# The second pointwise product of a Conformer layer: high and low activations side by side in one 512-column product, and two sums in the epilogue

## The chip, the core and the metric

The kernel runs as one program on one core of one Trainium2 chip. The metric is device time in microseconds (us), the median of the runs shown. A profile is one execution of the program, recorded by the hardware profiler.

The engines are written as in the profile: PE is TensorE (matmul), PEld its weight load, DVE is VectorE, ACT is ScalarE, POOL is GpSimd, SP issues the large DMAs. L189 is line 189 of the kernel's file before the change.

## The reference, cut to what matters

The reference is a backbone of two layers over 256 latent tokens and 256 context tokens of width 1024. Layer 0 mixes tokens with a Conformer convolution module, layer 1 with a bidirectional mLSTM; a squared-ReLU MLP follows each. The change is in the last line of the convolution module and the sum that follows it:

```
a = jax.nn.silu(layer_norm(a + b_dw, ln_g, ln_b))
return a @ w_pw2 + b_pw2                            # conformer_conv
...
h = layer_norm(ALPHA * h + g1 * y, ln1_g[i], ln1_b[i])
h = layer_norm(ALPHA * h + g2 * sq_relu_mlp(modulate(h, sh2, sc2), mlp_w1[i], mlp_w2[i]), ln2_g[i], ln2_b[i])
```

`a @ w_pw2` has 512 tokens in two streams (s = 0, the context, and s = 1, the latent tokens), 1024 inputs and 1024 outputs. The gate `g1` differs by stream.

## The kernel before, in words

**Layout.** Activations lie channel-first: a tile holds 128 channels in its partitions and the 512 tokens of both streams in its columns. `LO` is columns 0 to 255 and `HI` columns 256 to 511. `x[f]` (f = 0 to 7) is the residual.

**Splitting.** A product in full float32 precision is made from three products of a reduced type. `split` (L153) writes the high part of a value (a cast on ACT, L154) and the low part, the value less its high part (DVE, L155). `mm3` (L184) then issues three matmuls into one PSUM tile: high weight by high activation (L185), high weight by low activation (L188), low weight by high activation (L189). One output block of 128 channels over 1024 inputs is 8 k-tiles, so 24 matmuls.

**The stage of the change.** `silu` (L1112) makes the product's input for one stream: for each k-tile f two transposes on PE into a PSUM bank (L1119), the SiLU on ACT (L1122), a cast and a subtraction. The high part goes into columns `LO` of a tile of 512 columns and the low part into `HI` of the same tile (L1124, L1125); `sact[s]` keeps the two halves as a pair (L1126).

`gemm2_steps` (L292) makes the product, stream by stream, with eight output blocks m for each. In stream 0 the first four (`ko=4`) are made together, k-tile by k-tile, in halves of two banks opened ahead (L310 to L323). The other twelve, m = 4 to 7 of stream 0 and m = 0 to 7 of stream 1, are made one after the other (L324 to L330), each in one of the three banks with the tag "mm", of which it uses 256 columns. The weights are split once and kept: m = 0 to 3 in the tiles `wh` and `wl`, m = 4 to 7 in tiles of the pool "hid".

The epilogue `pw2_epi` (L1180) adds gate times product to the residual on DVE (L1181). It then feeds the result to the layer norm of that stream (`Norm`, L494): sums on DVE (L508, L510, L536, L538, L540), one early mean on PE (L514), a shift by it (L530), squares on ACT (L535). After the last block, `finish` (L543) makes the statistics: small matmuls on PE (L548, L551), a few tiny DVE instructions (L553 to L561), a square root on ACT (L558) and transposes on PE (L564). `apply` (L567) and `affine_half` (L588) then make the MLP's input `uu`, for each f two adds on DVE (L569, L570), two activations on ACT (L592) and a subtraction on DVE (L593).

The MLP's first product (`mlp`, L1195) runs through `gemm2_steps` as well, stream 0 first with three blocks together (`ko=3`), six blocks for each stream. Its inputs are the halves `LO` of `uu` for stream 0 and `HI` for stream 1. Its epilogue is L1202, L1203 and a split.

**What sets the order.** The text of the kernel doesn't set the order on an engine alone. The framework's scheduler orders each engine's instructions ahead of the run, by priorities and its own estimate of when operands are ready, unless an instruction is tied by hand (`tc.issue_after`, `tc.keep_in_program_order`). In this stage nothing on PE is tied, apart from a few statistics. The order is then fixed in the program: on the chip an engine waits at an instruction whose operands aren't there.

Of the kernel before, what the change touches and what calls it, by code (L numbers as in the profile page):

```python
# [12 lines left out]
ALU = mybir.AluOpType  # L13
# [8 lines left out]
C = 256  # L22
# [49 lines left out]
def hybrid_kernel(ctx: ExitStack, tc: tile.TileContext, xT, vecs_d, taps_d, bdw_d, ada0_w, ada_w, wg_d, pw1a, pw1, pw2, w1_0, w2_0,  # L72
                  w1_1, w2_1, up_x, up_z, wv, wo, bo_d, wk, wq, wqT, wdown, rows_d, out):
    nc = tc.nc
# [10 lines left out]
    def nm(s):  # L85
        uid[0] += 1
        return f"{s}_{uid[0]}"
# [3 lines left out]
    def tmp(tag, dt=F32):  # L91
        return tp.tile([P, T], dt, tag=tag, name=nm(tag), bufs={"E": 4, "S": 2, "L": 2, "F": 1}[tag])
# [8 lines left out]
    def psum(tag="mm"):  # L101
        return pp.tile([P, 512], F32, tag=tag, name=nm(tag), bufs={"mm": 3, "ln": 2, "fl": 1, "cv": 2}[tag])
# [16 lines left out]
    def V(name, i=0, n=1):  # L119
        o = _OFF[name][0]  # L120
        return vecs[:, o + i:o + i + n]
# [24 lines left out]
    def raw_load(src):  # L146
        raw = wp.tile([P, 2048], F32, tag="raw", name=nm("raw"), bufs=3)
        loaded[0] = nc.sync.dma_start(raw[:, :src.shape[-1]], src).ins
        return raw
# [3 lines left out]
    def split(hi, lo, src):  # L153
        c = nc.scalar.copy(hi, src)  # L154
        lastsub[0] = nc.vector.tensor_tensor(lo, src, hi.bitcast(F32), op=ALU.subtract).ins  # L155
        return c.ins
# [4 lines left out]
    def split_w(src, make=None):  # L161
        n = src.shape[-1]
        if make is not None:
            his, los = [], []
            for i in range(0, n, T):
                his.append(make(F32R))
                los.append(make(F32R))
                split(his[-1], los[-1], src[:, i:i + T])
            return his, los
        hi = wp.tile([P, 1024], F32R, tag="wh", name=nm("wh"), bufs=NW)[:, :n]  # L170
        lo = wp.tile([P, 1024], F32R, tag="wl", name=nm("wl"), bufs=NW)[:, :n]
        anchors.append(split(hi, lo, src))
        return hi, lo
# [10 lines left out]
    def mm3(ps, wh, wl, xh, xl, start, stop):  # L184
        a = nc.tensor.matmul(ps, wh, xh, start=start, stop=False)  # L185
        if pin[0]:
            tc.keep_in_program_order(a)
        nc.tensor.matmul(ps, wh, xl, start=False, stop=False)  # L188
        lastmm[0] = nc.tensor.matmul(ps, wl, xh, start=False, stop=stop).ins  # L189
# [3 lines left out]
    def mm_any(ps, wh, wl, r, start, stop):  # L193
# [10 lines left out]
        todo[0](start, False)  # L204
        todo[1](False, stop)

    def joined(ps):
        n = ps.shape[-1] // 2
        t = tmp("E")
        nc.scalar.copy(t[:, n:2 * n], ps[:, n:])  # L210
        nc.vector.tensor_tensor(t[:, :n], ps[:, :n], t[:, n:2 * n], op=ALU.add)
        return t[:, :n]
# [7 lines left out]
    def kcol(w, kt):  # L220
        if isinstance(w[0], list):
            w, kt = (w[0][kt // 4], w[1][kt // 4]), kt % 4
        return w[0][:, kt * P:(kt + 1) * P], w[1][:, kt * P:(kt + 1) * P]
# [64 lines left out]
    def gemm2(*a, **k):  # L288
        for _ in gemm2_steps(*a, **k):
            pass  # L290

    def gemm2_steps(w_ap, groups, rhs, order, epi, keep, ko=0, pre=None, again=None, two=None):  # L292

        ws = dict(pre or {})
        raws = {}

        def weights_of(m):
            if m not in ws:  # L300
                g = groups[m // 2]
                if g not in raws:
                    raws[g] = raw_load(w_ap[g, 0])
                ws[m] = split_w(raws[g][:, (m % 2) * 1024:(m % 2 + 1) * 1024], keep if m >= NW else None)
            return ws[m]

        for i, (s, sl) in enumerate(order):
            r = [(h_[:, sl], l_[:, sl]) for h_, l_ in rhs] if not isinstance(rhs, dict) else rhs[s]
            k0 = ko if i == 0 else 0
            if k0:  # L310
                if two:
                    pss = [two[m // 2][:, HALVES[m % 2][1]] for m in range(k0)]
                else:
                    pss = [psum("mm" if m < 3 else "cv")[:, :C] for m in range(k0)]
                for m in range(k0):
                    weights_of(m)
                for kt in range(8):
                    for m in range(k0):
                        mm3(pss[m], *kcol(ws[m], kt), *r[kt], kt == 0 and (not two or m % 2 == 0),
                            kt == 7 and (not two or m % 2 == 1))  # L320
                for m in range(k0):
                    epi(m, pss[m], s, sl)
                yield  # L323
            for m in again if i and again else range(k0, 2 * len(groups)):  # L324
                w = weights_of(m)
                ps = psum()[:, :C]
                for kt in range(8):
                    mm3(ps, *kcol(w, kt), *r[kt], kt == 0, kt == 7)
                epi(m, ps, s, sl)
                yield  # L330
# [138 lines left out]
    def ad(l, s, which):  # L469
        i = ["sh1", "sc1", "g1", "sh2", "sc2", "g2"].index(which)  # L470
        return ada[l][:, i * DT:(i + 1) * DT, s]
# [18 lines left out]
    LO, HI = slice(0, C), slice(C, T)  # L490
# [130 lines left out]
    x, u = [], []  # L621
# [98 lines left out]
    def silu():  # L720
        for i in range(2):
            keep(nc.vector.tensor_tensor(cs[:, :, 14 + i], sgc[:, i * DT:(i + 1) * DT], cc[:, i * DT:(i + 1) * DT],
                                         op=ALU.mult))
# [5 lines left out]
    two = lambda c: et[:, c:c + 2 * (HL + 1)].rearrange("p (i k) -> p i k", i=2)  # L729
# [268 lines left out]
    def apply_norm(pair, h):  # L998
        mv = pair_mv[pair]
        y, z = [Y[2 * pair + i][h] for i in range(2)]  # L1000
        nc.scalar.activation(y, y, AF.Identity, scale=mv[:, 0, 2:3], bias=mv[:, 0, 3:4])
        mark["norm", pair, h] = nc.vector.tensor_scalar(z, z, mv[:, 1, 2:3], mv[:, 1, 3:4],
                                                        op0=ALU.mult, op1=ALU.add).ins
# [106 lines left out]
    sact = {0: [], 1: []}  # L1110

    def silu(s):  # L1112
        apply_norm(s, 0)
        for f in range(DT):
            if f % 2 == 0:
                tr = psum("ln")
                for i in (1, 3, 0, 2):
                    k = f + i // 2
                    mark["turn", k] = nc.tensor.transpose(tr[:, i * P:(i + 1) * P],  # L1119
                                                          Y[2 * s + i % 2][k // 4][:, k % 4 * P:k % 4 * P + P], ident).ins  # L1120
            y = tmp("S")[:, LO]
            nc.scalar.activation(y, tr[:, f % 2 * C:f % 2 * C + C], AF.Silu, scale=V("cln_g", f),  # L1122
                                 bias=V("cln_b", f))
            t = U(F32R)  # L1124
            cast = split(t[:, LO], t[:, HI], y)  # L1125
            sact[s].append((t[:, LO], t[:, HI]))  # L1126
            if f == 0:
                with tc.issue_after(cast):
                    apply_norm(s, 1)
            yield  # L1130

    for _ in silu(0):
        pass
# [27 lines left out]
    def ln1_half(s, sl):  # L1161

        lnp[s].finish()
        if not cab:
            cab.extend(comb(0, "ln1_g0", "ln1_b0", "sc2", "sh2"))
        if s == 0:
            for f in range(DT):
                uu.append((U(F32R), U(F32R)))
                affine_half(uu[f][0][:, sl], uu[f][1][:, sl], lnp[s].apply(f), s, *cab, f)
        else:  # L1170
            uside.append(ln1_rest(sl))
# [6 lines left out]
            yield  # L1178

    def pw2_epi(m, ps, s, sl):  # L1180
        nc.vector.scalar_tensor_tensor(x[m][:, sl], ps, ad(0, s, "g1")[:, m:m + 1], x[m][:, sl],  # L1181
                                       op0=ALU.mult, op1=ALU.add)
        lnp[s].feed(x[m][:, sl])
        if m == 2 * 4 - 1:
            ln1_half(s, sl)
# [134 lines left out]
    for f in range(0, DT, 2):  # L1320
        t = tmp("S")
# [116 lines left out]
    def queries(h):  # L1438
        qq = []

        def q_epi(m, ps):
            if m < 2:
                flush()
            t = qd.tile([P, 2, QW], F32R, tag="qq", name=nm("qq"), bufs=8)
            split(t[:, 0, :C], t[:, 1, :C], joined(ps))
            split(t[:, 0, C:], t[:, 1, C:], rk[:, 4 * h + m, :])
            qq.append((t[:, 0, :], t[:, 1, :]))

        for i, _ in enumerate(gemm_steps(wq, range(2 * h, 2 * h + 2), xcl, T, q_epi, pre=preq)):
            if i % 2:  # L1450
                ada_n2.step()
        return qq
# [230 lines left out]
    for i in range(2):  # L1683
        rx = raw_load(xl_dr[i].rearrange("p b c -> p (b c)"))
        for j in range(8):
            t = XL(F32R)
# [325 lines left out]
    for c in range(4):  # L2012
# [25 lines left out]
        for k2 in range(4):  # L2038
            raw = raw_load(w2_1[4 * c + k2])
            for i in range(2):  # L2040
                kt = 2 * k2 + i
# [3 lines left out]
                w = split_w(raw[:, i * 1024:(i + 1) * 1024])  # L2045
                w = [[w_[:, sl] for sl in HF] for w_ in w]
# [6 lines left out]
        if last:  # L2053
# [13 lines left out]
            for q, sl in HALVES:  # L2067
                ps = psum()[:, :C]
# [103 lines left out]
```

## Time and profile before

| | |
|---|---|
| median of 3 runs | 1655.14 us (1654.32 to 1655.25) |
| the profiled execution's own time | 1655.04 us |
| its span, first to last instruction | 1653.3 us |
| PE busy | 1642.4 us, 99% of the span |
| PEld busy | 1353.4 us, 82% |
| DVE busy | 1066.2 us, 64% |
| ACT busy | 727.7 us, 44% |
| granted TensorE clock | 0.999 |

The last 1.7 us of the profiled execution's time lie around the span. Matmuls are pipelined: a matmul's recorded duration is longer than the distance to the next one, so the cost of a matmul in a stream of them is the distance from start to start. The stage of the change lies between 176 and 216 us of the span.

### The profile page before, as it was taken

What the parts mean: (1) busy time and instruction counts of PE and PEld (TensorE: products, weight loads), DVE (VectorE), ACT (ScalarE), POOL (GpSimd) and SP (SyncE); (2) the same over time, 40 slices, a digit from 0 to 9 for tenths busy, and PEclk for the clock granted to TensorE, in tenths of its full rate; (3) what the DMA queues carried; (4) which work ended last, traced back from release to release, by engine and by line L of the source; (5) the groups of instructions that cost most, each with busy time, mean ns of one, the idle gap of its engine ahead of it and who ended that gap; (6) DMA issues with size and microseconds to landing.
All of it is one profiled execution on the core that took longest, in us unless ns stands there. A gap on an engine that the chain in (4) does not pass through costs nothing.

```text
span 1653.3 us, 22664 instructions
## 1 busy us (share of the span) xinstructions
PE 1642.4 (99%) x8794; PEld 1353.4 (82%) x8794; DVE 1066.2 (64%) x1916; ACT 727.7 (44%) x1170; POOL 15.2 (1%) x67
## 2 busy tenths in 40 slices
PE   9999999999999999999999999999999999999998
PEld 6675998888888998877787899888888888878886
DVE  7786895656535776762254753553489776776677
ACT  4313662232324475641133533442478654555453
POOL 0000000000000000000000000000000000000001
PEclk9999999999999999999999999999999999999999
DMA  9766223444324066557775852553466555674552
GB/s 355 254 212 247 90 78 112 153 141 141 120 98 153 17 229 195 185 196 277 279 243 158 290 179 88 178 191 143 149 228 223 209 211 203 241 293 178 179 195 86
DMA packets 80204, 305.81 MB, mean 185 GB/s; under 512 B 11964, under 2 KB 30304, under 8 KB 50016
## 3 DMA queue, kind: packets, MB, share of 16 engines
q1 hardware_dynamic: 57632, 288.07, 49.4%
q10 hardware_dynamic: 22464, 16.30, 3.2%
q8 instruction: 69, 1.13, 0.3%
q14 instruction: 39, 0.32, 0.1%
HBM read 286.47 MB, written 17.86 MB: 184 GB/s over the span
## 4 chain that ended last, share of the span: by engine, by line
PE 98%; DVE 1%; ACT 0%; issue 0%; DVEq 0%
PE mm L185 18%; PE mm L188 17%; PE mm L189 17%; PE mm L200 7%; PE mm L216 4%; PE mm L218 4%; PE mm L217 4%; PE mm L201 4%; PE cv L216 2%; PE cv L218 2%; PE cv L217 2%; PE fl L342 2%; PE cv L967 1%; PE ln L185 1%; PE ln L217 1%; PE ln L188 1%
## 5 line engine op out<-in xcount | busy, mean ns | idle before, releaser
L155 DVE TENSOR_TENSOR wl<-raw,wh 128x1024 fp32r<-128x1024 f32 x344 | 418.7, 1221 | 246.6 <-ACT wh L154 244.6
L154 ACT CAST wh<-raw 128x1024 fp32r<-128x1024 f32 x344 | 358.7, 1051 | 478.5 <-PE mm L188 271.9
L188 PE MATMUL mm<-u,wh 128*128 128x512 f32 (+1 forms) x802 | 289.0, 360 | 0.0
L185 PE MATMUL mm<-u,wh 128*128 128x512 f32 (+1 forms) x674 | 240.9, 358 | 0.0
L189 PE MATMUL mm<-u,wl 128*128 128x512 f32 (+1 forms) x674 | 238.7, 354 | 0.0
L188 PEld LDWEIGHTS mm<-u,wh 128*128 128x128 f32 x802 | 151.5, 189 | 22.9 <-issue 1.1
L185 PEld LDWEIGHTS mm<-u,wh 128*128 128x128 f32 x674 | 127.3, 189 | 23.9 <-issue 5.1
L189 PEld LDWEIGHTS mm<-u,wl 128*128 128x128 f32 x674 | 127.4, 189 | 17.7
L216 PE MATMUL mm<-wh,xl 128*128 128x512 f32 x256 | 101.0, 395 | 0.1
L185 PE MATMUL mm<-xm,wh 128*128 128x512 f32 x256 | 101.0, 394 | 0.0
L217 PE MATMUL mm<-wh,xl 128*128 128x512 f32 x256 | 100.0, 391 | 0.0
L189 PE MATMUL mm<-xm,wl 128*128 128x512 f32 x256 | 99.7, 390 | 0.0
L218 PE MATMUL mm<-wl,xl 128*128 128x512 f32 x256 | 99.2, 391 | 0.1
L185 PE MATMUL mm<-hid,wh 128*128 128x512 f32 (+1 forms) x256 | 93.3, 365 | 0.0
L189 PE MATMUL mm<-hid,wl 128*128 128x512 f32 (+1 forms) x256 | 92.8, 363 | 0.0
L188 PE MATMUL mm<-hid,wh 128*128 128x512 f32 (+1 forms) x256 | 92.8, 363 | 0.0
L200 PE MATMUL mm<-x,wh 128*128 128x512 f32 x232 | 81.1, 398 | 0.0
L188 PE MATMUL mm<-qq,wh 128*128 128x272 f32 x256 | 73.9, 289 | 0.0
L185 PE MATMUL mm<-qq,wh 128*128 128x272 f32 x256 | 73.5, 289 | 0.0
L189 PE MATMUL mm<-qq,wl 128*128 128x272 f32 x256 | 73.5, 288 | 0.0
L1226 DVE SCALAR_TENSOR_TENSOR x<-mm,ada,x 128x256 f32<-128x256 f32 x64 | 28.5, 480 | 63.7 <-PE mm L189 63.7
L200 PE MATMUL mm<-u,wh 128*128 128x512 f32 x192 | 68.6, 398 | 0.0
(567 smaller groups left out, 3274.6 us busy)
## 6 DMA issues: line engine op xcount, KB each, us to landing
raw<-w SPq DMA_DIRECT2D x64, 1024.0 KB, 4.8
raw<-wo SPq DMA_DIRECT2D x32, 1024.0 KB, 4.8
raw<-ada_w SPq DMA_DIRECT2D x23, 1024.0 KB, 5.2
ar<-ada_w SPq DMA_DIRECT2D x80, 256.0 KB, 3.9
raw<-wv SPq DMA_DIRECT2D x16, 1024.0 KB, 7.0
raw<-wqT SPq DMA_DIRECT2D x16, 1024.0 KB, 5.8
raw<-wq SPq DMA_DIRECT2D x16, 1024.0 KB, 5.2
raw<-wk SPq DMA_DIRECT2D x16, 1024.0 KB, 4.9
```

The lines of the kernel that those rows point to most:

```text
L154: c = nc.scalar.copy(hi, src)
L155: lastsub[0] = nc.vector.tensor_tensor(lo, src, hi.bitcast(F32), op=ALU.subtract).ins
L185: a = nc.tensor.matmul(ps, wh, xh, start=start, stop=False)
L188: nc.tensor.matmul(ps, wh, xl, start=False, stop=False)
L189: lastmm[0] = nc.tensor.matmul(ps, wl, xh, start=False, stop=stop).ins
L200: todo = [lambda s_, e_: nc.tensor.matmul(ps, wh, r[0], start=s_, stop=e_), lambda s_, e_: nc.tensor.matmul(ps[:, :n], wl, r[0][:, :n], st ...
L201: lambda s_, e_: nc.tensor.matmul(ps[:, :n], wl, r[0][:, :n], start=s_, stop=e_)]
L216: nc.tensor.matmul(ps, xh, wh, start=start, stop=False)
L217: nc.tensor.matmul(ps, xl, wh, start=False, stop=False)
L218: nc.tensor.matmul(ps, xh, wl, start=False, stop=stop)
L342: a = mark_unit[0] = nc.tensor.matmul(ps[32 * j:32 * j + 32], cs[:, kt, 14 - 2 * v:46 - 2 * v], blocks[kt], start=first and kt < 4, stop=l ...
L1226: nc.vector.scalar_tensor_tensor(res[m][:, sl_], p_, g[:, m:m + 1], res[m][:, sl_], op0=ALU.mult, op1=ALU.add)
```

## The change

In twelve of the sixteen outputs the two matmuls by the high weight become one of 512 columns, whose moving operand is the whole tile with the high part on the left and the low part on the right. The low weight by the high part stays a matmul of 256 columns, into the left half of the same bank. An output is then 8 matmuls of 512 and 8 of 256 columns, in the order four wide, eight narrow, four wide. The bank holds two partial sums, in its two halves, which the epilogue adds to the residual by two instructions, one after the other. The four outputs that are made together keep the old form.

```
+    def wide(ps, w, r, start, stop):
+
+        n = r[0][0].shape[-1] // 2
+        seq = [(0, kt) for kt in range(4)] + [(1, kt) for kt in range(8)] + [(0, kt) for kt in range(4, 8)]
+        for i, (low, kt) in enumerate(seq):
+            w_, x_, o_ = kcol(w, kt)[low], r[kt][0], ps
+            if low:
+                x_, o_ = x_[:, :n], ps[:, :n]
+            nc.tensor.matmul(o_, w_, x_, start=start and i == 0, stop=stop and i == 15)
...
                 for kt in range(8):
                     for m in range(k0):
-                        mm3(pss[m], *kcol(ws[m], kt), *r[kt], kt == 0 and (not two or m % 2 == 0),
+                        x_ = r[kt] if len(r[kt]) == 2 else [r[kt][0][:, h_] for h_ in (LO, HI)]
+                        mm3(pss[m], *kcol(ws[m], kt), *x_, kt == 0 and (not two or m % 2 == 0),
...
                 w = weights_of(m)
+                if len(r[0]) == 1:
+                    ps = psum()
+                    wide(ps, w, r, True, True)
+                    epi(m, ps, s, sl)
+                    yield
+                    continue
                 ps = psum()[:, :C]
...
-            sact[s].append((t[:, LO], t[:, HI]))
+            sact[s].append((t,))
...
     def pw2_epi(m, ps, s, sl):
-        nc.vector.scalar_tensor_tensor(x[m][:, sl], ps, ad(0, s, "g1")[:, m:m + 1], x[m][:, sl],
-                                       op0=ALU.mult, op1=ALU.add)
+        for h_ in (LO, HI)[:ps.shape[-1] // C]:
+            nc.vector.scalar_tensor_tensor(x[m][:, sl], ps[:, h_], ad(0, s, "g1")[:, m:m + 1], x[m][:, sl],
+                                           op0=ALU.mult, op1=ALU.add)
```

## The prediction

> **What bounds the kernel now.** I read the page's busy shares first, then the chain of work that ended last, then a table of the stage in stretches.
>
> ```profile
> PE 1642.4 (99%) x8794; PEld 1353.4 (82%) x8794; DVE 1066.2 (64%) x1916; ACT 727.7 (44%) x1170; POOL 15.2 (1%) x67
> ...
> PE 98%; DVE 1%; ACT 0%; issue 0%; DVEq 0%
> ```
>
> PE carries 98% of the chain: what a matmul costs in a stream of matmuls is what the kernel costs, unless PE is made to wait. PE and PEld have the same count, so each matmul has its own weight load, also where two in a row use the same weights. The shares are averages, so the stage is read by itself: four blocks of stream 0, blocks 0 to 3 of stream 1, blocks 4 to 7, the MLP's six blocks on stream 0, and the start of its blocks on stream 1.
>
> ```profile
> core 0: us, PE busy (x) PEld busy (x) DVE busy (x) ACT busy (x) POOL busy (x), PEclk, DMA share, GB/s
> 176.28:190.15 13.87, 13.87 (x117) 13.65 (x115) 12.35 (x42) 10.39 (x26) 0.00 (x0) 1.00 0.30 121
> 190.15:203.67 13.52, 13.25 (x111) 12.90 (x109) 10.83 (x29) 8.29 (x13) 0.00 (x0) 1.00 0.14 45
> 203.67:215.69 12.02, 12.02 (x101) 11.95 (x99) 11.52 (x34) 9.24 (x20) 0.00 (x0) 1.00 0.10 40
> 215.69:234.45 18.76, 18.76 (x159) 18.72 (x157) 16.93 (x46) 11.38 (x27) 0.00 (x0) 1.00 0.32 113
> 234.45:246.00 11.55, 11.55 (x99) 11.55 (x98) 11.00 (x26) 8.33 (x17) 0.00 (x0) 1.00 0.10 28
> ```
>
> The columns are the stretch, its length, and each engine's busy time. PE is full but for 0.27 us in the second row. DVE is nearly full too: it has 1.52, 2.69, 0.50, 1.83 and 0.55 us free. So the stage has two engines near their limit, and the change takes work from the one and gives work to the other.
>
> **PE: what a block saves.** The cost of a matmul is the distance from start to start.
>
> ```profile
> 203.67 0.28 PE L185 MATMUL mm<-u,hid 128*128 128x256 f32 x1
> ...
> 206.55 0.28 PE L185 MATMUL mm<-u,hid 128*128 128x256 f32 x1
> ...
> 209.94 0.28 PE L185 MATMUL mm<-u,hid 128*128 128x256 f32 x1
> ...
> 700.02 0.39 PE L185 MATMUL mm<-u,wh 128*128 128x512 f32 x1
> ...
> 703.88 0.39 PE L189 MATMUL mm<-u,wl 128*128 128x512 f32 x1
> ...
> 909.18 0.39 PE L200 MATMUL mm<-u,wh 128*128 128x512 f32 x1
> 909.41 0.27 PE L201 MATMUL mm<-u,wl 128*128 128x256 f32 x1
> ...
> 915.07 0.40 PE L200 MATMUL mm<-u,wh 128*128 128x512 f32 x1
> ```
>
> The first two rows are the starts of two neighbouring blocks of this product: 24 matmuls of 256 columns in 2.88 us, 0.120 us each. Between 700.02 and 703.88 lie 17 steps of matmuls of 512 columns: 3.86 / 17 = 0.227 us. Twice 0.120 is 0.240, so a pair made into one saves 0.013 us: the columns stay, the fixed part of one matmul goes. The new block is 8 x 0.227 + 8 x 0.120 = 2.776 us. The last three rows check that from another stage that already mixes the forms: 17 pairs of one wide and one narrow in 5.89 us, 0.3465 us a pair, 2.772 us for eight. A block saves 0.104 to 0.108 us, twelve save 1.25 to 1.30 us; I take 1.25. That is the whole of what the change can bring by itself.
>
> The Trainium skill, "TensorE: Matmul & The Clock Gate", section "Back-to-back issue gap", speaks against the size of this gain: its gap for a warm matmul is its columns at 2.4 GHz plus about 2.5 ns. By it 96 matmuls fewer save an estimated 0.24 us. The rows here say 13 ns for each, so the sum goes by the rows.
>
> **DVE: what a block adds.** One more instruction of the form L1181 for each of the twelve blocks. It can't cost less than nothing, since no instruction of DVE goes.
>
> ```profile
> L1181 DVE SCALAR_TENSOR_TENSOR x<-mm,ada,x x14: 475/478/485, 176.3 to 217.6; 128x256 f32<-128x256 f32 x14
> ...
> 191.05 0.48 DVE L1181 SCALAR_TENSOR_TENSOR x<-mm,ada,x 128x256 f32<-128x256 f32 x1
> 191.56 0.42 DVE L530 TENSOR_TENSOR x<-x,ln 128x256 f32<-128x256 f32 x1
> ...
> 206.54 0.48 DVE L1181 SCALAR_TENSOR_TENSOR x<-mm,ada,x 128x256 f32<-128x256 f32 x1
> 206.93 0.42 DVE L593 TENSOR_TENSOR u<-S,u 128x256 fp32r<-128x256 f32 x1
> ```
>
> Each lasts 0.478 us. Where the next instruction needs nothing of it, that starts 0.39 us later (206.54 to 206.93); where it needs the result, as the shift L530 does, 0.51 us later. The second sum needs the first. So the price is 0.39 us each if the scheduler puts something between, 0.51 us if not: 4.7 to 6.1 us for twelve. I take 4.8, the lower end, since DVE has other work queued in all of the stage.
>
> The Trainium skill, "VectorE: DVE Perf Modes", section "The DRAIN you can't avoid", has a rule against such a second instruction: the next operation doesn't start until the pipeline is empty, so the count of operations is what to keep low. By it each would cost its full 0.478 us whatever follows, 5.7 us for twelve. The 0.39 us of the unrelated pair disagrees; the 0.51 us of the dependent pair goes with it.
>
> **Where DVE's added time ends up.** DVE isn't the chain, so the 4.8 us cost only what reaches PE. Behind a second sum wait, on DVE, the layer-norm steps, the weight subtractions and the MLP's input; PE waits for these.
>
> ```profile
> 181.63 0.42 DVE L155 TENSOR_TENSOR u<-S,u 128x256 fp32r<-128x256 f32 x1 [0.88 <-ACT u L154]
> 182.64 0.42 DVE L155 TENSOR_TENSOR u<-S,u 128x256 fp32r<-128x256 f32 x1 [0.58 <-ACT u L154]
> ...
> 194.10 0.16 DVE L553 COPY lc<-ln 128x4 f32<-128x4 f32 x1 [1.21 <-PE ln L551]
> ...
> 195.52 1.28 ACT L558 ACT_TABLE_LOAD   x1
> 196.81 0.30 ACT L558 ACTIVATE lc<-lc,eps 128x2 f32<-128x2 f32 x1
> ...
> 193.04 0.24 PE L548 MATMUL ln<-inv_c,ln 128*128 128x1 f32 x1 [0.21 <-DVE ln L536]
> ...
> 217.55 0.48 DVE L1181 SCALAR_TENSOR_TENSOR x<-mm,ada,x 128x256 f32<-128x256 f32 x1
> ...
> 218.09 0.39 PE L185 MATMUL mm<-u,wh 128*128 128x256 f32 x1
> ...
> 237.45 0.28 PE L188 MATMUL mm<-u,wh 128*128 128x256 f32 x1
> ...
> 237.71 0.42 DVE L593 TENSOR_TENSOR u<-S,u 128x256 fp32r<-128x256 f32 x1
> ```
>
> Stream 0, four blocks, +1.6 us on DVE: the idle 0.88 and 0.58 us (181.63, 182.64) lie behind the first block's sum and take in some 1.5 us of work, but only that of blocks queued before them. The other sums delay the end of the first layer norm by about 1 us. There PE already waits 0.21 us (193.04), and it comes 0.4 us earlier: this is the first place for a stall, up to 1.4 us if the order stays. Behind it the delay is mostly hidden: the square root needs the table load that ends at 196.81 (195.52 plus 1.28), while the tiny instructions before it start at 194.10 and would be done by then even 1 us later.
>
> Stream 1, eight blocks, +3.2 us: from 190.15 to 203.67 DVE has 2.69 us free, a part of them the 1.21 us of the round trip over PE, and from 203.67 to 215.69 0.50 us. Of the 4.8 us I count 1.5 as taken in before 190.15, 1 to 2 in the second stretch, 0.5 in the third: 1 to 2 us are left when the stage ends.
>
> Three things on PE wait for that. First the bank: a bank is held up to 0.51 us longer, but blocks go round three banks, and the block whose sum starts at 206.54 hands its bank to the block at 209.94: 206.54 + 0.48 leaves 2.9 us, less the delay. Second, the bank of the last block: its sum ends at 217.55 + 0.48 = 218.03, and a matmul that starts late and long follows at 218.09, which fits a third block of the MLP waiting for it. Third the MLP's input for stream 1: its last part is done at 237.71 + 0.42 = 238.13, while PE is already among the blocks that use it and runs an L188 (237.45) ahead of its L185. So in a fixed order there is no margin in the second and the third. But the order isn't fixed by the kernel: the scheduler makes it anew for the changed program, and the lone L188 shows that it puts other blocks' matmuls before those whose operands come late. With three banks it has three blocks of 2.88 us to choose from, more than the 1 to 2 us of delay.
>
> So I take 0.5 us of new waits, between 0 and 1.5. The transposes, ACT's instructions and the DMAs stay in number; SP and POOL get nothing. The narrow product of the last k-tile comes sooner in its block (after 4 x 0.227 + 7 x 0.120 = 1.75 us in place of 21 x 0.120 = 2.52), but it needs only the high part, which ACT makes ahead of DVE's subtraction; I cost it at nothing.
>
> **The sum.** 1655.04 us (span 1653.3 and 1.74 around it) - 1.25 + 0.5 = 1654.3 us. The median of the runs shown, 1655.14, is 0.1 us above the profiled execution, so the sum holds for it as well. A measurement of this kernel can tell about 0.2% from no change, 3.3 us: the forecast is no difference.
>
> **The rivals.**
>
> *DVE's free time is no room, and the slower engine sets the end.* The idle stretches are round trips (over ACT at 181.63, over PE at 194.10): work ahead of them pushes them back. Then the 4.8 us arrive whole at the MLP's input for stream 1, less the 0.55 us free in the last row of the table: 238.13 moves by 4.25 us, PE stands there, and its own 1.25 us are lost in the wait: 1655.04 + 4.25 = 1659.3 us; at 6.1 us 1660.6. It counts as slower from 3.3 us of delay. For it: there is no margin at 218.03 and 238.13, and DVE has 0.50 us free of 12.02 just before. Against it: the idle 0.88 and 0.58 us come right behind the first added sum, the table load hides a delay, and a new order can fill in. Chance 0.15. In a milder form 1 to 2.5 us arrive: 1656.0 to 1657.5 us, within the 0.2%; chance 0.10.
>
> *The fixed part doesn't go.* If 512 columns behind new weights here cost twice 256, PE gains only the 0.24 us: 1655.04 - 0.24 + 0.5 = 1655.3 us. Against it stand two stages with 0.227 us. This is also what the TensorE page's gap would make of it. Chance 0.08.
>
> *A new order elsewhere.* The scheduler's estimates shift from here on, and later choices with them. PE is idle for 1653.3 - 1642.4 = 10.9 us in all, so a luckier order could bring a few us, to about 1651; an unluckier one costs as much. Nothing in the profile says which. Chance 0.07: 0.05 for the better side, 0.02 for the worse.
>
> **How the numbers follow.** Forecast 0.60, 1653.75 to 1655.3 us, as the waits are 0 to 1.5. Within 0.2%: 0.60 + 0.10 + 0.08 = 0.78; slower 0.15 + 0.02 = 0.17; faster 0.05. The range goes from 1653.0, the full gain with part of PE's few waits gone as well, to 1659.3, the centre of the rival on the slower side; beyond it lie half of that rival and the unlucky orders, under it the lucky ones, some 0.15 in all.
>
> **What would show it right or wrong.** Right: in the twelve blocks wide matmuls step by 0.227 us and narrow ones by 0.120, and a block takes 2.78 us; twelve more sums of 0.48 us on DVE; the MLP's first blocks start about 1 us earlier; the statistics of the second layer norm come 1 to 2 us later; PE's waits between 190 and 246 us grow by under 1.5 us, and behind that the kernel runs as before. Wrong: a PE wait of over 2 us on DVE near the second layer norm or the MLP's stream 1, steps of 0.240 us, or a difference that arises after 260 us.

## The result and the profile after

The changed kernel takes 1657.83 us (median of 20 executions, 1655.87 to 1659.16); the kernel before took 1654.82 (20, 1654.16 to 1655.73). The ratio is 1.0017, 95% interval 1.0011 to 1.0023: 3.0 us slower, where the sum had 0.8 us faster. That is just inside the 0.2% that the prediction calls no difference, but the interval excludes 1, and the median lies outside the forecast of 1653.75 to 1655.3 us (inside its wide range, 1653.0 to 1659.3). The profiled execution took 1656.66 us, span 1654.9.

First the page: busy times, and the chain of work that ended last.

```profile
PE 1641.3 (99%) x8698; PEld 1347.5 (81%) x8698; DVE 1069.7 (65%) x1928; ACT 727.8 (44%) x1170; POOL 15.2 (1%) x67
...
PE 94%; DVE 2%; DMA 2%; ACT 1%; issue 0%; SPq 0%; DVEq 0%; ACTq 0%
```

The 96 matmuls are gone, the twelve sums are there, PE is busy for 1.1 us less. But the chain now leaves PE: DVE, the DMAs and ACT have 2, 2 and 1% of it. Next the stage in stretches, with the same columns and the same work in each row as before; the fourth row is new.

```profile
core 0: us, PE busy (x) PEld busy (x) DVE busy (x) ACT busy (x) POOL busy (x), PEclk, DMA share, GB/s
175.88:189.45 13.57, 13.57 (x84) 11.80 (x83) 12.36 (x42) 9.96 (x25) 0.00 (x0) 1.00 0.30 124
189.45:201.95 12.50, 12.50 (x78) 11.06 (x76) 11.66 (x30) 5.87 (x8) 0.00 (x0) 1.00 0.18 61
201.95:213.72 11.77, 11.77 (x67) 10.00 (x65) 11.43 (x34) 10.74 (x22) 0.00 (x0) 1.00 0.07 27
213.72:215.70 1.98, 0.00 (x1) 0.03 (x1) 1.98 (x7) 1.06 (x3) 0.00 (x0) 1.00 0.00 0
215.70:234.40 18.70, 18.70 (x156) 18.68 (x157) 17.28 (x49) 11.24 (x27) 0.00 (x0) 1.00 0.29 113
```

The three stretches of the product take 37.84 us; before they took 13.87 + 13.52 + 12.02 = 39.41. So PE does the product 1.57 us faster, near the forecast 1.25 and the 0.27 us that it was idle before. Then it stands for 1.98 us. With the MLP's 0.06 us (18.76 to 18.70) the stage comes out 0.35 us longer. What PE waits for is a bank; DVE's instructions and then PE's show it:

```profile
207.22 0.47 DVE L1199 SCALAR_TENSOR_TENSOR x<-mm,ada,x 128x256 f32<-128x256 f32 x1
...
208.61 0.47 DVE L1199 SCALAR_TENSOR_TENSOR x<-mm,ada,x 128x256 f32<-128x256 f32 x1
209.00 0.41 DVE L587 TENSOR_TENSOR x<-x,ln 128x256 f32<-128x256 f32 x1
...
213.34 0.42 DVE L610 TENSOR_TENSOR u<-S,u 128x256 fp32r<-128x256 f32 x1
...
214.35 0.47 DVE L1199 SCALAR_TENSOR_TENSOR x<-mm,ada,x 128x256 f32<-128x256 f32 x1
214.74 0.41 DVE L553 TENSOR_TENSOR ln<-ln,L 128x256 f32<-128x256 f32 x1
215.07 0.47 DVE L1199 SCALAR_TENSOR_TENSOR x<-mm,ada,x 128x256 f32<-128x256 f32 x1
```

```profile
215.70 0.36 PE L185 MATMUL mm<-u,wh 128*128 128x256 f32 x1 [1.98 <-DVE x L1199]
```

L1199 is the sum (L1181 before), L587 and L610 are steps of the MLP's input (L570 and L593 before). Block 4 of stream 1 is summed at 207.22 and 208.61, block 5 only at 214.35 and 215.07, though by four blocks of 2.78 us from 201.95 its product is there at about 207.5 (an estimate). Between them DVE works off the MLP's input and steps of the second layer norm without a gap. Then blocks 5, 6 and 7 hold all three banks, and the MLP's first matmul stands until block 5's second sum is done. In before, DVE has the sums of blocks 4 and 5 done by 210.62 (209.51 + 1.11), ahead of the last step of the MLP's input for stream 0:

```profile
209.51 1.11 DVE L1181 SCALAR_TENSOR_TENSOR x<-mm,ada,x 128x256 f32<-128x256 f32 x2
210.54 0.42 DVE L593 TENSOR_TENSOR u<-S,u 128x256 fp32r<-128x256 f32 x1
```

In after that step (213.34) is 2.8 us later, and the sums of block 5 come behind it. So DVE is later, and the scheduler has also moved these sums back. No run holds DVE's order fixed, so how the 1.98 us divide between the two isn't shown.

Compared matmul by matmul, PE's delay against before stays within 0.4 us from there to 1100 us. It then grows by some 2 us, nearly all of it at two places, around 1240 us (0.8) and around 1404 us (1.2). At the larger one ACT waits for a DMA and PE for ACT. ACT and PE of after, then ACT of before:

```profile
1404.69 1.99 ACT L154 CAST wh<-raw 128x1024 fp32r<-128x1024 f32 x2 [2.13 <-DMA raw<-wo]
```

```profile
1405.79 0.50 PE L226 MATMUL mm<-wh,xl 128*128 128x512 f32 x1 [0.80 <-ACT wh L154]
```

```profile
1402.68 1.05 ACT L154 CAST wh<-raw 128x1024 fp32r<-128x1024 f32 x1 [0.81 <-DMA raw<-wo]
```

The order of PE's, DVE's and ACT's instructions is that of before everywhere outside the stage, and POOL's and SP's throughout. So no new order made this loss. What differs is in the DMA view; a queue's row gives packets, MB and share, and the last number of a load's row is the time from issue to landing. First after, the packets of 1401 to 1402 us and the load that ACT waits for, issued at 1398.5; then before, the packets of 1406 to 1407.2 us, the same load, issued at 1397.8, and the next one, issued at 1402.4.

```profile
q8 instruction: 1, 0.02, 5.9%
...
raw<-wo SPq DMA_DIRECT2D x1, 1024.0 KB, 6.1
```

```profile
q8 instruction: 1, 0.02, 5.1%
...
raw<-wo SPq DMA_DIRECT2D x1, 1024.0 KB, 4.7
...
raw<-wo SPq DMA_DIRECT2D x1, 1024.0 KB, 4.8
```

In after, a packet of the queue q8 comes in the middle of the load, which lands after 6.1 us. In before the packet comes 5 us later, at the very end of the next load, and neither load is late. Around 1240 us it is alike: the load there lands after 6.3 us in after and 5.2 in before. Over the whole run q8 moves 68 packets of 16 KB (69 before), which fits PE's instructions in blocks of 256: a matmul and its weight load are two, so 2 x 8698 / 256 = 67.95 and 2 x 8794 / 256 = 68.7. So 192 instructions fewer in the stage shift every later border of a block by 192 instructions, and with it the time at which the next block is fetched.

### The profile page after: what moved, and what is told of

Its sections match the earlier page's. It is cut to its first block, busy times and chain, and to the rows that moved or that the text cites. A ratio compares the mean times of both kernels' runs of the same rounds, so it can differ in the third digit from the quotient of the medians.

```text
span 1654.9 us, 22487 instructions
## 1 busy us (share of the span) xinstructions
PE 1641.3 (99%) x8698; PEld 1347.5 (81%) x8698; DVE 1069.7 (65%) x1928; ACT 727.8 (44%) x1170; POOL 15.2 (1%) x67
## 3 DMA queue, kind: packets, MB, share of 16 engines
q8 instruction: 68, 1.11, 0.3%
## 4 chain that ended last, share of the span: by engine, by line
PE 94%; DVE 2%; DMA 2%; ACT 1%; issue 0%; SPq 0%; DVEq 0%; ACTq 0%
PE mm L185 17%; PE mm L188 17%; PE mm L189 17%; PE mm L200 7%; PE mm L201 4%; PE mm L226 3%; PE mm L228 3%; PE mm L227 3%; PE cv L226 2%; PE cv L228 1%; PE cv L227 1%; PE fl L359 1%; PE mm L215 1%; PE cv L984 1%; PE ln L185 1%; PE ln L188 1%
## 5 line engine op out<-in xcount | busy, mean ns | idle before, releaser
L188 PE MATMUL mm<-u,wh 128*128 128x512 f32 (+1 forms) x770 | 280.0, 364 | 0.0
L185 PE MATMUL mm<-u,wh 128*128 128x512 f32 (+1 forms) x642 | 231.5, 362 | 2.0 <-DVE x L1199 2.0
L189 PE MATMUL mm<-u,wl 128*128 128x512 f32 (+1 forms) x642 | 229.7, 358 | 0.0
L188 PEld LDWEIGHTS mm<-u,wh 128*128 128x128 f32 x770 | 145.4, 189 | 23.0 <-issue 1.1
L185 PEld LDWEIGHTS mm<-u,wh 128*128 128x128 f32 x642 | 121.0, 189 | 26.4 <-issue 5.5
L189 PEld LDWEIGHTS mm<-u,wl 128*128 128x128 f32 x642 | 121.3, 189 | 17.5
L188 PE MATMUL mm<-hid,wh 128*128 128x512 f32 (+1 forms) x256 | 92.8, 363 | 0.0
L188 PE MATMUL mm<-qq,wh 128*128 128x272 f32 x256 | 73.9, 289 | 0.0
```

## The experiments

Three theories. **S**: the second sums make DVE late, and it holds the banks; this is the loss in the stage. **F**: the late loss comes from the borders of PE's instruction blocks, a fetch of which now falls into a weight load. **T**, its rival: the late loss follows from being late, or from any shift of PE against the DMAs. In the table "stage" and "late" are the change of PE's delay against before across the stage, and from 600 to 1500 us, in the one profiled execution. A single profile moves by itself: before run again lost 0.87 us late, 0.66 of it near 840 us, where no other run loses as much. The phase is the number of PE instructions added to before, modulo 256. "Load" is the landing time of the weight load that ACT waits for around 1404 us, with a star where a packet of q8 comes in its middle.

| kernel | us, before beside it | ratio, 95% interval | stage | late | phase | load |
|---|---|---|---|---|---|---|
| one_sum | 1654.58, 1654.85 | 0.9998 (0.9988 to 1.0007) | -1.79 | +3.13 | 64 | 6.1* |
| old_two_sums | 1654.92, 1654.85 | 1.0000 (0.9992 to 1.0009) | +0.77 | -0.06 | 0 | 4.7 |
| before_halve32 | 1656.71, 1654.85 | 1.0012 (1.0003 to 1.0020) | | +2.06 | 64 | 6.0* |
| after_halve96 | 1656.99, 1654.85 | 1.0015 (1.0006 to 1.0024) | +0.4 | +0.50 | 0 | 4.9 |
| cv_banks | 1657.24, 1654.76 | 1.0015 (1.0006 to 1.0023) | +0.50 | +2.5 | 64 | 6.1* |
| wide8 | 1655.51, 1654.76 | 1.0006 (0.9997 to 1.0015) | -0.81 | +3.4 | 128 | 4.7 |
| before_halve128 | 1656.70, 1654.76 | 1.0012 (1.0003 to 1.0021) | | +0.3 | 0 | 4.8 |
| before_halve96 | 1656.53, 1654.76 | 1.0010 (1.0001 to 1.0019) | | +0.2 | 192 | 4.7 |
| wide4 | 1653.76, 1654.63 | 0.9994 (0.9985 to 1.0003) | -0.66 | 0.0 | 192 | 4.7 |
| act_sum | 1659.27, 1654.63 | 1.0028 (1.0017 to 1.0039) | +2.4 | +2.3 | 64 | 6.2* |
| after_again | 1657.36, 1654.63 | 1.0015 (1.0006 to 1.0024) | +1.8 | +2.6 | 64 | 6.1* |
| before_again | 1654.58, 1654.63 | 0.9999 (0.9990 to 1.0008) | | +0.87 | 0 | 4.9 |

**one_sum: after without the second sums.** The right half of the bank (high weight by low activation) is left out of the residual.

```
-        for h_ in (LO, HI)[:ps.shape[-1] // C]:
+        for h_ in (LO,):
```

> The changed kernel with the first of the two epilogue sums alone: the right half of the bank (high weight by low activation) is left out of the residual in twelve blocks, so DVE has no added instruction while PE has all 96 matmuls fewer. Theory S (the second sums hold the banks; the 1.98 us wait of PE at 215.70 is theirs): that wait falls under 0.3 us and the stage ends 1 to 1.3 us earlier than in the kernel before. Theory F (the other loss, some 1.7 us that the profile shows at 1111, 1238 and 1403 us, comes from PE's instruction blocks, which are fetched at other moments because PE has 192 instructions fewer): the late loss stays, so the median is 0 to 1.5 us above the kernel before. Rival T (the late loss follows from the delay in this stage): no late loss, median 1.0 to 1.3 us below the kernel before.

PE gains 1.79 us in the stage and no wait is left there; the MLP's first matmul starts right behind the last block:

```profile
211.65 2.27 PE L215 MATMUL mm<-u,hid 128*128 128x512 f32 x13
213.76 0.28 PE L185 MATMUL mm<-u,wh 128*128 128x256 f32 x1
```

So PE's gain is real, and the twelve sums cost 0.35 + 1.79 = 2.1 us on PE, not 0.5. The late loss is there all the same, though this kernel is ahead when it gets there: being late is not its cause. 1.1 us of it, near 1296 us, comes in no other run; a load with a packet of q8 in it (`raw<-v_dr`) lands after 7.5 us there. The late loss takes the gain back, and the median ends at that of before, not 0 to 1.5 us above it; the profiled execution is the slowest of the eleven, so a late loss of 3.1 us isn't the usual one.

**old_two_sums: before, with the sum issued twice in the twelve blocks.** The product is counted twice there.

```
+        for _ in range(1 if s == 0 and m < 4 else 2):
             nc.vector.scalar_tensor_tensor(x[m][:, sl], ps, ad(0, s, "g1")[:, m:m + 1], x[m][:, sl],
```

> The kernel before with its 24 matmuls of 256 columns, and the epilogue's sum issued twice in the same twelve blocks (the product counts twice there). DVE has the change's twelve added instructions, PE has its old count. Theory S: PE comes 1.25 us later to the last blocks, so the bank wait is smaller, 0.5 to 1.5 us, and the stage costs that much. Theory F: nothing more is lost later, median 0.5 to 1.5 us above the kernel before. Rival T: the late loss follows a delay in the stage, median 2 to 3 us above.

The sums alone cost PE 0.77 us in the stage, with one wait of 1.1 us on the sum, and nothing later. The median doesn't show them: it is that of before, where 0.5 to 1.5 us more was expected. With the old product PE comes to the MLP later, so less of DVE's lateness shows: that PE's saving uncovers the rest is argued from this.

**before_halve32: before, with 32 matmuls of 512 columns in the MLP behind the stage made as two halves.** This adds 64 PE instructions and leaves the stage alone: the borders of the blocks behind it lie as in after.

```
-        nc.tensor.matmul(ps, wh, xl, start=False, stop=False)
+        halves = (LO, HI) if halve[0] > 0 and ps.shape[-1] == T else (slice(None),)
+        halve[0] -= len(halves) - 1
+        for h_ in halves:
+            nc.tensor.matmul(ps[:, h_], wh, xl[:, h_], start=False, stop=False)
```

> The kernel before, with 32 matmuls of 512 columns each made as two of 256 in the MLP's second product of layer 0, right behind the stage. That adds 32 weight loads and 32 matmuls, 64 instructions on PE, which puts the borders of PE's instruction blocks (256 instructions) where the changed kernel has them from there on, with nothing else of the change. By the rows of 0.120 and 0.227 us it costs 32 x 0.013 = 0.42 us by itself. Theory F: the late loss comes here too, median 1.5 to 3 us above the kernel before. Rivals S alone and T: median 0.4 us above.

The halves themselves cost 0.54 us, 17 ns each. The late loss is there, 2.06 us, at the same two places, with neither a wide product nor a second sum. Its ACT and PE around 1404 us read like those of after:

```profile
1404.95 2.00 ACT L154 CAST wh<-raw 128x1024 fp32r<-128x1024 f32 x2 [2.10 <-DMA raw<-wo]
```

```profile
1406.05 0.50 PE L220 MATMUL mm<-wh,xl 128*128 128x512 f32 x1 [0.78 <-ACT wh L154]
```

**after_halve96: after, with 96 such matmuls halved.** PE then has as many instructions as before, and the borders are back where they were. The edit is that of before_halve32 with 96 for 32.

> The changed kernel with 96 matmuls of 512 columns each made as two of 256 in the MLP's second product of layer 0: 192 instructions on PE are back, and the borders of its instruction blocks lie behind that point where they lie in the kernel before. Its price is 96 x 0.013 = 1.25 us. Theory F: the late loss goes, median 1.3 to 2 us above the kernel before, below the changed kernel. Rivals S alone and T: the median of the changed kernel and 1.25 us, some 4.2 us above the kernel before.

The halves cost 1.6 us and the stage 0.4 as in after, but the late loss is 0.5 us, less than before shows against itself. ACT and the load around 1404 us are back too:

```profile
1404.93 1.05 ACT L154 CAST wh<-raw 128x1024 fp32r<-128x1024 f32 x1 [0.92 <-DMA raw<-wo]
```

```profile
raw<-wo SPq DMA_DIRECT2D x1, 1024.0 KB, 4.9
```

**before_halve96 and before_halve128: before, with 96 and 128 matmuls halved.** The first is the price of after_halve96's halves without the change, the second a whole block of 256 instructions. The edits differ from before_halve32's in the number alone.

> The kernel before with 96 matmuls of 512 columns each made as two of 256 in the same place: 192 more instructions, borders 64 instructions off on the other side than with 32 halved. Own price 96 x 0.013 = 1.25 us. Theory F: the late loss is another one than the 2.1 us of 32 halved, and comes at other places than 1230 and 1403 us; median between 1.25 and 4 us above the kernel before. Rival T: loss at the same places as with 32 halved, median about 3.4 us above.

> The kernel before with 128 matmuls of 512 columns each made as two of 256 in the MLP's second product of layer 0: 256 more instructions on PE, one whole block, so the borders stand where they stood, while PE's later work comes 128 x 0.013 = 1.7 us later. Theory F: no late loss beyond that, median 1.3 to 2.2 us above the kernel before. Rival T (any shift of PE's work in time, or any added instruction, brings the late loss that 32 halved matmuls brought): 3.2 to 4 us above.

Both are later than before_halve32 when they come to 1200 us (by 1.1 and 1.4 us) and lose 0.2 and 0.3 us late. So it isn't the delay, and not that there are more instructions: T falls. These two ran on another chip than before_halve32; cv_banks (below), on the same chip as they, has the late loss, so the chip isn't the cause. For before_halve96, F had expected a late loss at other places; there is none. Every kernel of phase 64 loses 2.1 to 3.1 us late, in six profiles with after's two; those of phase 0 and 192 lose 0.9 at most, and 0.4 at most behind 1100 us. The load around 1400 us lands after 6.0 to 6.2 us in the six profiles in which a packet of q8 comes in its middle, and after 4.7 to 4.9 us in the other eight. Each against before beside it, after_halve96 is 2.14 us slower and before_halve96 1.77. The 0.37 us between them would be the change at a harmless phase, like its 0.4 us in the stage, but each interval is wider than that.

**cv_banks: after, with the last two blocks of stream 1 in banks of the tag "cv".**

```
-                    ps = psum()
+                    ps = psum("cv" if i and m > 5 else "mm")
```

> The changed kernel with blocks 6 and 7 of stream 1 in the two banks of the tag cv, which stand empty then, in place of two of the three mm banks. Nothing else is changed. Theory S (the second sums hold the banks that the MLP's first blocks need): PE's wait of 1.98 us falls under 0.3 us, and the stage ends 0.8 to 1.8 us earlier than in the changed kernel. Theory F (late loss from the borders of PE's instruction blocks, which are 192 instructions off as in the changed kernel): the loss of 2 to 3 us behind 1100 us stays. Together: median 0 to 1.5 us above the kernel before. If the wait only moves to the MLP's input (the order rival of the prediction): the stage stays within 0.4 us of the changed kernel's and the median about 2.5 us above.

The wait for the bank goes, and up to 225 us PE gains 1.7 us on before. But the stage ends with a loss of 0.50 us: PE loses 2.2 us from there to 240 us on the MLP's input for stream 1. DVE and then PE:

```profile
232.57 0.42 DVE L610 TENSOR_TENSOR u<-S,u 128x256 fp32r<-128x256 f32 x1
232.91 0.42 DVE L587 TENSOR_TENSOR x<-x,ln 128x256 f32<-128x256 f32 x1
233.24 0.41 DVE L586 TENSOR_TENSOR x<-x,ln 128x256 f32<-128x256 f32 x1
233.57 0.42 DVE L610 TENSOR_TENSOR u<-S,u 128x256 fp32r<-128x256 f32 x1
...
234.56 0.42 DVE L610 TENSOR_TENSOR u<-S,u 128x256 fp32r<-128x256 f32 x1
```

```profile
233.04 0.39 PE L188 MATMUL mm<-u,wh 128*128 128x256 f32 x1
...
234.04 0.39 PE L188 MATMUL mm<-u,wh 128*128 128x256 f32 x1
...
235.04 0.39 PE L188 MATMUL mm<-u,wh 128*128 128x256 f32 x1
```

L610 makes the low part of one k-tile, and L188 is the matmul that needs it. Three of each are shown. L188 starts 0.47 or 0.48 us after an L610, and they are 1.00 us apart: PE goes at DVE's pace of three instructions a k-tile. No wait is listed at these rows, as each gap is short; the step shows it. DVE is the bound of these blocks, and without the bank's wait its lateness shows here.

**wide8 and wide4: the wide product, with its two sums, in the first eight and the first four of the twelve blocks alone.** The other blocks keep the old product and one sum.

```
-                if len(r[0]) == 1:
+                if len(r[0]) == 1 and (i == 0 or m < 4):     # wide8; wide4: and i == 0
...
-                    mm3(ps, *kcol(w, kt), *r[kt], kt == 0, kt == 7)
+                    x_ = r[kt] if len(r[kt]) == 2 else [r[kt][0][:, h_] for h_ in (LO, HI)]
+                    mm3(ps, *kcol(w, kt), *x_, kt == 0, kt == 7)
```

> The wide product and the two sums in the first eight of the twelve blocks alone (4 to 7 of stream 0, 0 to 3 of stream 1); the last four of stream 1 as in the kernel before. PE saves 8 x 0.104 = 0.83 us, DVE has eight added sums. Theory S: the sums behind which the MLP's banks come free are those of the last four blocks, so the bank wait falls to under 0.8 us, and the stage is even with the kernel before or up to 0.8 us better. Theory F: the borders of PE's blocks are 128 instructions off, which no run has shown; the late loss is what that gives, somewhere from 0 to 3 us, and it is the same 2 to 3 us if any shift brings it.

> The wide product and the two sums in blocks 4 to 7 of stream 0 alone, where DVE had 1.52 us free in the kernel before; all of stream 1 as before. PE saves 4 x 0.104 = 0.42 us. Theory S: no bank wait, since the last four blocks' sums are single; the stage is 0.4 to 0.8 us better than in the kernel before. Theory F: PE has 64 instructions fewer, which puts the borders of its blocks where 96 halved matmuls put them in the kernel before, and that run showed no late loss: median 0.2 to 0.9 us below the kernel before. Rival T (any shift brings the late loss): 1.5 to 2.5 us above.

The stage brings 0.66 us with four blocks, 0.81 with eight (a wait of 0.5 us on the bank is left), and costs 0.35 with twelve: DVE had room for the first four blocks' sums, little for the next four's and none for the last four's. wide4 has no late loss either, and its load around 1400 us lands after 4.7 us. It is the lowest of all, 0.9 us below before, but its interval takes in 1. One of its eleven executions took 5035.3 us; it isn't in the interval, and nothing shows why. wide8 loses 3.4 us late, 1.1 us around 1240 us and 1.9 us at another place, where PE waits until 1209.3 us for the mLSTM's forget gates. A fetch lies ahead of each, at 1219.5 and at 1192.3 us. The one at 1192.3 comes in a load that lands after 7.1 us (4.8 in after), and ACT, whose next work is a step of those gates, waits for it; wide8, then before:

```profile
1198.94 2.00 ACT L154 CAST wh<-raw 128x1024 fp32r<-128x1024 f32 x2 [3.59 <-DMA raw<-wo]
```

```profile
1198.04 2.00 ACT L154 CAST wh<-raw 128x1024 fp32r<-128x1024 f32 x2 [1.27 <-DMA raw<-wo]
```

That is the same mechanism at another load. No run with that phase and no change was made, so for phase 128 it rests on this profile; its executions lie wide apart, 1653.73 to 1659.58 us.

**act_sum: after, with the second sum made by ACT (gate times right half) and added on POOL.** DVE is back at its 1916 instructions.

```
+        if ps.shape[-1] > C:
+            e_ = tmp("E")[:, :C]
+            nc.scalar.activation(e_, ps[:, HI], AF.Identity, scale=ad(0, s, "g1")[:, m:m + 1])
+            nc.gpsimd.tensor_tensor(x[m][:, sl], x[m][:, sl], e_, op=ALU.add)
+        nc.vector.scalar_tensor_tensor(x[m][:, sl], ps[:, LO], ad(0, s, "g1")[:, m:m + 1], x[m][:, sl],
+                                       op0=ALU.mult, op1=ALU.add)
```

> The changed kernel, all twelve blocks wide, with the second sum off DVE: ACT scales the right half of the bank by the gate into SBUF, GpSimd adds that to the residual, and DVE adds the left half as the kernel before did its one sum. DVE has its old count. Theory S (DVE, not the form of the product, is what loses PE's gain in this stage): the stage ends 0.8 to 1.8 us earlier than in the kernel before, if ACT and GpSimd keep up. Theory F: the borders are those of the changed kernel, so the late loss of 2 to 3 us stays: median 0.3 to 2 us above the kernel before.

It is worse, 1659.27 us. POOL's instructions in the stage, and PE's waits there:

```profile
L1201 POOL TENSOR_TENSOR x<-x,E 128x256 f32<-128x256 f32 x12 | 10.4, 868 | 149.6 <-ACT E L1200 147.1 <-DVE x L586 2.5
```

```profile
PE mm L215 <- ACT u L154: 1.3, 1, 1.3
PE mm L215 <- DVE x L1202: 1.1, 1, 1.1
PE ln L565 <- DVE ln L553: 0.3, 1, 0.3
PE mm L185 <- DVE x L1202: 0.2, 1, 0.2
```

ACT, which splits the second stream's activations, is now late itself (1.3 us), and the first sum on DVE stands behind ACT and 0.87 us of POOL. The product now waits 1.1 us for a bank. ACT and GpSimd don't keep up, so this run doesn't say what the stage would be with DVE relieved.

**after_again and before_again: both kernels unchanged, run beside wide4 and act_sum.**

> The changed kernel once more, unchanged, for a second profile and its spread. The fetch of one of PE's instruction blocks falls again at 1401 to 1402.5 us, inside the load of the output gate's weights, with a wait of over 2 us on ACT there; late loss 2 to 3.5 us; median 2 to 3.3 us above the kernel before.

> The kernel before once more, unchanged, for a second profile. The fetch falls at 1406 to 1407 us, between two loads; no late loss against the first profile over 0.5 us; the median of the runs before.

The medians repeat: 2.8 us between them here, 3.0 in the result. The fetches come somewhat later than expected, at 1403.6 us in after_again, whose load moved with it, and at 1407.7 in before_again, in the last half microsecond of the next load; and before_again's 0.87 us late is above the 0.5. The profile of after_again shows a third loss: its stage costs 1.8 us, not 0.35. Its windows behind the same wait:

```profile
214.00:216.00 2.00, 0.02 (x1) 0.06 (x1) 2.00 (x7) 1.06 (x3) 0.00 (x0) 1.00 0.00 0
216.00:217.00 1.00, 1.00 (x6) 1.00 (x7) 1.00 (x4) 0.41 (x1) 0.00 (x0) 0.69 0.00 0
217.00:218.00 1.00, 1.00 (x7) 1.00 (x6) 1.00 (x4) 0.01 (x1) 0.00 (x0) 0.50 0.00 0
218.00:219.00 1.00, 1.00 (x7) 1.00 (x7) 1.00 (x4) 0.23 (x1) 0.00 (x0) 0.50 0.00 0
219.00:220.00 1.00, 1.00 (x7) 1.00 (x7) 1.00 (x5) 0.19 (x1) 0.00 (x0) 0.60 0.00 0
220.00:221.00 1.00, 1.00 (x10) 1.00 (x10) 1.00 (x2) 0.83 (x2) 0.00 (x0) 1.00 0.00 0
```

PE stands for 1.99 us, and then the granted clock (third column from the end) falls to half. The four rows lack 0.31, 0.50, 0.50 and 0.40 of it, so half clock lasted 1.71 / 0.50 = 3.4 us. In the first profile of the same kernel the clock stayed at 1.00 behind the same wait (the row from 215.70). So the same bank wait costs 2 us in one execution and 1.5 us more in another.

## Why the prediction was wrong

**PE's saving was right.** Rows of after, wide, narrow, wide:

```profile
191.31 2.00 PE L215 MATMUL mm<-u,wh 128*128 128x512 f32 x8
193.15 1.12 PE L215 MATMUL mm<-u,wl 128*128 128x256 f32 x8
194.11 0.63 PE L215 MATMUL mm<-u,wh 128*128 128x512 f32 x2
```

Eight wide take 1.84 us (0.23 each), eight narrow 0.96 (0.120). one_sum shows the whole: 1.79 us, the 1.25 of the sum, the 0.27 us idle before, and some 0.3 us that isn't traced. The rival "the fixed part doesn't go" is excluded.

**DVE's price per sum was right.** The sum at 214.35 is followed at 214.74: 0.39 us, against a duration of 0.47. The scheduler did put other work between the two sums of nearly every block.

**"So I take 0.5 us of new waits, between 0 and 1.5" failed.** It was 1.98 us on a bank, at the MLP's first block: between the first of the three places named (a bank handed on after three blocks) and the second (the last block's bank, at the MLP's third block). The step that failed is "With three banks it has three blocks of 2.88 us to choose from, more than the 1 to 2 us of delay". All three banks were held by blocks whose sums were queued, so there was no bank for any block to be put ahead. The 2.9 us of margin of the first place was also no margin for the last blocks: block 5's sums run some 7 us after its product. That DVE's order could move them so far back wasn't asked. And cv_banks shows that the third place waits behind the bank: without the bank wait PE loses 2.2 us on the MLP's input. In the prediction's terms the waits were to be 0 to 1.5 us against a gain of 1.25, at most 0.25 us net; the stage came out at 0.35 us, and at 1.8 with the half clock of after_again, which the prediction didn't have. So the rival "DVE's free time is no room" had the mechanism right, that of DVE's added time more reaches PE than was taken (2.1 us by one_sum). Its milder form asks for 1 to 2.5 us net, which the stage reaches only with the half clock; its full form, 4.25 us, isn't reached.

**"Behind that the kernel runs as before" failed.** The text names "a difference that arises after 260 us" as a sign of being wrong, and most of the loss does: 2.0 us in the profile of after. The rival "a new order elsewhere" doesn't explain it, as the order there is the same. What did it was not in the prediction at all: 192 PE instructions fewer move the fetches of PE's instruction blocks, one of them into a weight load that PE waits for. The prediction took the DMAs as unchanged since they stay in number, and so put this at nothing. That the phase decides is shown (phase 64 against 0 and 192, with and without the change). That fetch and load get in each other's way on the DMA engines is argued from the landing time, 6.0 us and more against 4.9 at most. That the median still lies inside the wide range (1653.0 to 1659.3) is luck: some 2 us of it come from a term that the sum doesn't have.

**The sum as it was.** Between the two profiles: -0.40 with which PE comes to the stage, -1.57 for its work there, +1.98 for the bank, -0.06 in the MLP, -0.36 from there to 1100 us (a wait of 0.3 us that before has near 550 us is gone), +2.0 late: 1.6 us, the difference of the spans. The median lies 1.2 us above the profiled execution, where before's lies 0.2 below its own; the half clock behind the bank wait fits that size. Every execution's mean clock is on record, to three places, and 3.4 us at half clock take 0.001 off it. The five of after's executions at 0.999, the profiled one among them, took 1656.4 us on average, the fifteen at 0.998 and 0.997 took 1658.1; of before's executions beside the experiments none is under 0.998, and those at 0.999 and 0.998 differ by 0.2 us at most. So the half clock probably falls in most executions of after. That is argued from the third place of a mean; two profiles alone show after's clock from moment to moment.

## What to carry to other kernels

Before work moves to a second engine that is nearly full, ask what its late instructions hold, and where the scheduler may put them: here they held three banks, and no order of PE's could get round those. Make such a change only where that engine has room (four of the twelve blocks here), and count a wait of PE at more than its length. When a change takes out or adds PE instructions, compare it also at the same count modulo the instruction block, by a pad elsewhere whose price is measured alone, before a difference of a tenth of a per cent is put down to the edit.

## What the runs showed of the hardware that was not expected

- **A fetch of instructions can delay a weight load.** Judging by the number of packets, PE's instructions come on q8, 16 KB at a time, 68 to 70 times in a run. With one in its middle the 1 MB load around 1400 us landed after 6.0 to 6.2 us, in six profiles, and else after 4.7 to 4.9 us, in the eight others; in after ACT then waited 2.1 us, in before 0.8. A packet at the very end of a load cost nothing (4.8 us in before).
- **A wait of 2 us can halve the clock.** The granted clock fell to 0.50 behind 1.99 us without matmuls in one execution, and stayed at 1.00 behind 1.98 us in another, and behind 1.9 us in wide8. The Trainium skill, "TensorE: Matmul & The Clock Gate", section "What's actually happening", has the clock drop after at least one idle window of about 3.4 us, and calls the window free-running. The wait here is shorter than that window and the clock still fell; the stretch at half clock, 3.4 us, is its length.
- **Halving a matmul of 512 columns costs 17 ns** (0.54 us for 32, 1.6 for 96), near the 13 ns that the rows of 256 and 512 columns give for a pair made into one.
